# A decoder step on one Trainium2 core: the RWKV-7 chunk inverses' substitution on GpSimd, and projections in another order

## The chip, the core and the metric

The kernel runs on one core of a Trainium2 chip. The time is that of the whole kernel in device microseconds, from one launch. TensorE (PE) multiplies matrices, VectorE (DVE), ScalarE (ACT) and GpSimd (POOL) work element by element on 128 partitions, SyncE (SP) issues most DMAs. Each engine takes its own instructions strictly in order; between engines semaphores set what waits for what.

## What is computed

The reference is one inference step of a decoder of two layers (width 1024) on 512 prompt tokens and 8 x 4 sample tokens, 544 columns in all. Each layer has a SwiGLU block, a mixer and a second SwiGLU block. The mixer of the second (odd) layer is the one that the change touches: one input projection feeds a dilated window attention (8 heads: q, k, v) and an RWKV-7 time mixer (8 heads of 64). Cut to what matters:

```python
p = h @ odd_w_in[o]                       # q, k, v of the attention, then r, k, v, w, a, g of RWKV-7
def step(s, inp):                         # one token of RWKV-7, per head, s is 64 x 64
    r_t, w_t, k_t, v_t, kk_t, a_t = inp
    sk = jnp.einsum('bhvk,bhk->bhv', s, kk_t)
    s = (s * w_t[:, :, None, :] - sk[..., None] * (kk_t * a_t)[:, :, None, :]
         + v_t[..., None] * k_t[:, :, None, :])
    return s, jnp.einsum('bhvk,bhk->bhv', s, r_t)
s_final, ys = lax.scan(step, s0, seq)
...
mix = jnp.concatenate([att, yd], -1) @ odd_w_out[o]
```

All values are float32. A float32 matmul is made from three matmuls of split operands (high x high, high x low, low x high).

## The kernel before

**Projections.** A strip is 128 output columns; its weight of 1024 x 128 comes by DMA as `raw` (L446), ScalarE rounds it to `wh` (L448), VectorE takes the rest `wl` (L449), and TensorE runs three matmuls for each of 8 slices of the inner dimension, once for each half of the 544 columns (L460 to L462). So a half strip is 24 matmuls of 128 x 272. In the odd mixer there are 14 strips of RWKV-7 (x0 to x3 is r of the four head pairs, x4 to x7 is k, x8 to x11 is v, x12 and x13 the low-rank inputs; functions `xmixes`, `xmix`), 4 slices of v of the attention (`vproj`, two half strips each, turned by L575 and L578 afterwards), and 4 groups hp of q and k (`odd_qk`, four half strips each).

**RWKV-7 in chunks.** The 512 prompt tokens are taken as 16 chunks of 32. The heads go in four pairs p = 0 to 3. For each pair the generator `rw_first(p)` does three parts, split by `yield`: decays, k and its norm; then the scaled vectors Q (from kk), R (from r) and KBf, and the chunk matrices MQ and GP (matmuls L1422, masks L1425), of which the part to be inverted goes through DRAM (`rab`) into `EA`, so that each of the 128 partitions holds one chunk of 32 x 32 in an order that suits; then the **substitution**: 31 steps of a multiply (L1440, into `rtm`) and a subtract (L1441) on `U`, each step on the result of the one before. U goes back through DRAM (`rtb`) into `TT`. Between the two, the third part also turns Q and KBf and projects v of the pair (x8+p), whose chunk form `rv` has one buffer, as `EA`, `U`, `MQ` and `KBf` have; `rtm` and the strips' border tile `pdb` have two.

`rw_inverse(p)` then multiplies with the inverse (first matmul L1498, which needs TT, QB, VU), and builds per chunk the transition `MT` (L1517, into a diagonal that GpSimd has written, L1449), the input `W`, the readout `RR` (L1526, onto a copy of R that GpSimd has made, L1448) and Y. After two pairs `rw_rec(g)` runs through the 16 chunks (L1544), and `rw_sample(p)` does the sample tokens.

**The order.** The body of `odd_mix` names the order p by p: the first parts of pair p+1, the third part of pair p, the second part of pair p+1, some groups of `odd_qk`, the inverse of pair p. A scheduler orders each engine's instructions by the order in which they are written (an earlier one has priority) and by when their operands and buffers come free, so instructions of several pairs stand interleaved on an engine. v of the attention is projected ahead of all pairs, its first slice within the low-rank part.

Of the kernel before, what the change touches and what calls it, by code (L numbers as in the profile page):

```python
# [26 lines left out]
class Kern:  # L27
# [1224 lines left out]
    def rw_setup(self, pL, pA, pE, p2, pJ):  # L1252
# [83 lines left out]
    def rw_first(self, p):  # L1336
# [49 lines left out]
        t = E()  # L1386
# [23 lines left out]
        V.tensor_tensor(chunks(QR[:, 1]), chunks(r), dv[:, :, 1:33], op=M)  # L1410
# [5 lines left out]
        for h2 in range(2):  # L1416
# [19 lines left out]
        for i in range(31):  # L1436
# [3 lines left out]
            V.tensor_tensor(tv, U[:, 0:nj, i:i + 1].to_broadcast([128, nj, 31 - i]), EA[:, i:i + 1, i + 1:32].to_broadcast([128, nj, 31 - i]), op=M)  # L1440
            V.tensor_tensor(U[:, 0:nj, i + 1:32], U[:, 0:nj, i + 1:32], tv, op=S)  # L1441
# [9 lines left out]
        self.turn(QB[:, 0], [QR[:, 0, 128 * i:128 * i + 128] for i in range(4)])  # L1451
# [20 lines left out]
        self.f[p] = QB, KB, VU, GP  # L1472
# [9 lines left out]
    def rw_inverse(self, p, QB, KB, VU, GP, kind="rs"):  # L1482
# [50 lines left out]
    def rw_rec(self, g, pool, pq):  # L1533
# [6 lines left out]
        for n in range(1, 16):  # L1540
# [479 lines left out]
```

## Time and profile before

| | us |
|---|---|
| three runs | 2569.62, 2573.84, 2588.95 |
| median | 2573.84 |
| profiled execution | 2567.64 |
| its span on the core | 2565.8 |
| TensorE busy | 2442.6 (95%) |
| VectorE busy | 1232.4 (48%) |
| ScalarE busy | 943.3 (37%) |
| GpSimd busy | 409.0 (16%) |

The span is that of the trace, from the first instruction to the last; the profiled execution is one run and has its own time. Busy times of TensorE are modelled ends of pipelined matmuls. "PEclk" is the clock that TensorE was granted, as a share of the full one. The odd mixer's part with the four pairs lies between about 1643 and 1957 us. A row of the timeline gives the start in the span, the duration, the engine, the line, what it writes and reads, and in brackets how long the engine was idle before and what ended it.

### The profile page before, as it was taken

To read this page: it belongs to the slowest core of one execution; us is meant where nothing else is said; L and a number is where in the kernel's file an instruction comes from. 1 tells how busy PE (TensorE), PEld (TensorE's weight loads), DVE (VectorE), ACT (ScalarE), POOL (GpSimd) and SP (SyncE) were. 2 spreads that over 40 slices of the span, in tenths; PEclk is the share of its full clock that TensorE was granted. 3 is DMA by queue.
4 is the path that set the end of the run, shared out by engine and by line. 5 is a ranking of instruction groups with operands and counts; after the bars stand their busy time and mean duration, and the time that the engine had idled before them with its cause. 6 is when DMAs were issued, how large, how long until landed. Compare 5 with 4: busy or idle time off the path is not lost.

```text
span 2565.8 us, 50682 instructions
## 1 busy us (share of the span) xinstructions
PE 2442.6 (95%) x20338; PEld 2253.4 (88%) x20338; DVE 1232.4 (48%) x2999; ACT 943.3 (37%) x2051; POOL 409.0 (16%) x616
## 2 busy tenths in 40 slices
PE   6999999899899999999999999889999999999996
PEld 4988999897588999999989999878877578999996
DVE  6532356544577333345423334558664567333343
ACT  4322323435555333224323322545422545333222
POOL 1000016411432000031000003312111122000032
PEclk8999999999999999999999999889988999999998
DMA  7666335567632222223562232322322632222221
GB/s 237 203 217 216 113 118 112 188 216 252 222 122 75 87 88 94 80 80 105 173 222 83 85 91 81 103 77 78 92 75 92 211 113 74 87 89 94 80 80 58
DMA packets 184027, 318.27 MB, mean 124 GB/s; under 512 B 38416, under 2 KB 47040, under 8 KB 183664
## 3 DMA queue, kind: packets, MB, share of 16 engines
q1 hardware_dynamic: 172096, 282.52, 34.6%
q0 software_dynamic: 10400, 31.06, 4.1%
q8 instruction: 159, 2.61, 0.4%
q10 hardware_dynamic: 1296, 1.46, 0.2%
q14 instruction: 76, 0.62, 0.1%
HBM read 288.68 MB, written 26.28 MB: 123 GB/s over the span
## 4 chain that ended last, share of the span: by engine, by line
PE 82%; DVE 7%; DMA 4%; ACT 4%; issue 1%; POOL 1%; SPq 1%; ACTq 0%; POOLq 0%; DVEq 0%
PE mm L460 23%; PE mm L462 23%; PE mm L461 22%; PE ps L185 2%; DVE x L347 1%; DMA ar<-in_ada_w 1%; DMA raw<-in_ada_w 1%; ACT t L249 1%; DVE wl L449 1%; PE sc L1178 1%; PE sc L1156 1%; PE ad L185 1%; PE ps L460 1%; PE ps L462 1%; PE ps L461 1%
## 5 line engine op out<-in xcount | busy, mean ns | idle before, releaser
L460 PE MATMUL mm<-xh,wh 128*128 128x272 f32 x3720 | 1089.4, 295 | 35.5 <-ACT xh L250 10.1
L461 PE MATMUL mm<-xl,wh 128*128 128x272 f32 x3720 | 1082.7, 291 | 2.0 <-DVE xl L251 2.0
L462 PE MATMUL mm<-xh,wl 128*128 128x272 f32 x3720 | 1083.0, 292 | 0.8 <-DVE wl L449 0.8
L460 PEld LDWEIGHTS mm<-xh,wh 128*128 128x128 f32 x3720 | 706.0, 190 | 85.2 <-ACT t L401 31.2
L449 DVE TENSOR_TENSOR wl<-raw,wh 128x512 fp32r<-128x512 f32 (+1 forms) x664 | 458.8, 703 | 537.0 <-ACT wh L448 505.0
L461 PEld LDWEIGHTS mm<-xl,wh 128*128 128x128 f32 x3720 | 710.5, 191 | 7.0 <-DVE xl L251 2.5
L462 PEld LDWEIGHTS mm<-xh,wl 128*128 128x128 f32 x3720 | 706.6, 190 | 7.8 <-issue 4.2
L448 ACT ACTIVATE wh<-raw 128x512 fp32r<-128x512 f32 (+1 forms) x664 | 401.5, 618 | 727.6 <-PE mm L461 565.9
L460 PE MATMUL mm<-hh,wh 128*128 128x272 f32 x1280 | 370.4, 289 | 0.0
L462 PE MATMUL mm<-hh,wl 128*128 128x272 f32 x1280 | 370.4, 289 | 0.0
L461 PE MATMUL mm<-hl,wh 128*128 128x272 f32 x1280 | 369.5, 289 | 0.0
L460 PEld LDWEIGHTS mm<-hh,wh 128*128 128x128 f32 x1280 | 241.4, 189 | 0.8 <-issue 0.4
L461 PEld LDWEIGHTS mm<-hl,wh 128*128 128x128 f32 x1280 | 241.2, 188 | 0.4
L462 PEld LDWEIGHTS mm<-hh,wl 128*128 128x128 f32 x1280 | 241.1, 188 | 0.4
L402 DVE TENSOR_TENSOR t<-t,mm 128x272 f32<-128x272 f32 x169 | 73.4, 434 | 279.6 <-ACT t L401 279.4
L401 ACT ACTIVATE t<-mm 128x272 f32<-128x272 f32 x169 | 65.6, 388 | 318.6 <-PE mm L462 318.6
L297 POOL TENSOR_TENSOR sa<-x 128x272 f32<-128x272 f32 x24 | 26.1, 1087 | 907.4 <-DVE x L291 852.0
L291 DVE SCALAR_TENSOR_TENSOR x<-mm,rg,x 128x272 f32<-128x272 f32 (+1 forms) x96 | 45.9, 479 | 171.4 <-PE mm L462 170.7
L466 DVE TENSOR_TENSOR hl<-t,hh 128x272 fp32r<-128x272 f32 x160 | 69.6, 439 | 35.8 <-ACT hh L465 35.3
L465 ACT ACTIVATE hh<-t 128x272 fp32r<-128x272 f32 x160 | 67.5, 426 | 38.5 <-DVE t L402 38.5
L277 POOL TENSOR_TENSOR sq<-sq,t 128x272 f32<-128x272 f32 x60 | 54.7, 926 | 18.1 <-ACT t L276 17.3
L249 ACT ACTIVATE t<-x,S,G 128x272 f32<-128x272 f32 (+1 forms) x80 | 44.5, 589 | 24.1 <-DVE x L348 23.5
(643 smaller groups left out, 2536.6 us busy)
## 6 DMA issues: line engine op xcount, KB each, us to landing
raw<-in_ada_w SPq DMA_DIRECT2D x192, 256.0 KB
raw<-in_wg SPq DMA_DIRECT2D x176, 256.0 KB
raw<-in_wu SPq DMA_DIRECT2D x176, 256.0 KB
raw<-in_wd SPq DMA_DIRECT2D x160, 256.0 KB
ar<-in_ada_w SPq DMA_DIRECT2D x96, 256.0 KB
raw<-in_odd_rw SPq DMA_DIRECT2D x28, 256.0 KB
xs<-x POOLq DMA_DIRECT2D x16, 272.0 KB, 4.0
x<-xs POOLq DMA_DIRECT2D x8, 544.0 KB, 7.8
```

The source lines that it names most:

```text
L185: return nc.tensor.matmul(ps[32 * j:32 * j + 32], self.c32[:, 9 * k:9 * k + 32], r, start=(k == 0), stop=(k == 7))
L249: nc.scalar.activation(t[:, 0:n], x[:, d, c0:pe], AF.Identity, scale=G[:, d, 0:1], bias=S[:, d, 0:1])
L277: G.tensor_tensor(s["q"], s["q"], t, op=A)
L401: self.act = nc.scalar.activation(s, pss[2 * i], AF.Silu)
L402: mul = nc.vector.tensor_tensor(s, s, pss[2 * i + 1], op=ALU.mult)
L448: nc.scalar.activation(wh[:, 0:w], r[:, 0:w], AF.Copy)
L449: (lo or nc.vector).tensor_tensor(wl[:, 0:w], r[:, 0:w], wh[:, 0:w].bitcast(F32), op=ALU.subtract)
L460: nc.tensor.matmul(ps, wh[:, s], mh, start=first, stop=False)
L461: nc.tensor.matmul(ps, wh[:, s], ml, start=False, stop=False)
L462: self.last = nc.tensor.matmul(ps, wl[:, s], mh, start=False, stop=last)
L465: self.nc.scalar.activation(hi, src, AF.Copy)
L466: return (lo_eng or self.nc.vector).tensor_tensor(lo, src, hi.bitcast(F32), op=ALU.subtract)
```

## The change

1. The 62 instructions of the substitution of each pair are issued to GpSimd (G) instead of VectorE (V).
2. The copy of R into RR is gone. Q and R stand in a ring of three slots, R in slot 0 or 2, and the addition L1526 reads R from there. 
3. GpSimd's product that writes the diagonal MT moves from the third part of `rw_first` to the head of `rw_inverse`, and the buffers of a group of two pairs are taken there.
4. v of the attention is no longer projected ahead of the pairs: 0, 1, 1 and 2 of its four slices are drawn in pairs 0 to 3, and its output DMAs go behind. The groups of q and k move by one pair: none, 0, 1, 2 instead of 0, 1, none, 2.
5. The chunk loop of `rw_rec` is written under a higher priority.
6. The pool of scratch tiles has 8 buffers instead of 9, and one scratch tile (t) takes the place of `cum`, which is dead by then.

Other lines move by one: L1441 and L1442 are the substitution of the changed kernel, L1499 the first matmul of the inverse.

```diff
-        t = E()
+        t = cum
...
-        QR = pJ.tile([128, 2, SP], F32, name="rQR")
+        Q, R, QR = self.RQR[:, 1], self.RQR[:, 2 * (p % 2)], self.RQR[:, p % 2:p % 2 + 2]
...
-            V.tensor_tensor(tv, U[:, 0:nj, i:i + 1].to_broadcast([128, nj, 31 - i]), EA[:, i:i + 1, i + 1:32].to_broadcast([128, nj, 31 - i]), op=M)
-            V.tensor_tensor(U[:, 0:nj, i + 1:32], U[:, 0:nj, i + 1:32], tv, op=S)
+            G.tensor_tensor(tv, U[:, 0:nj, i:i + 1].to_broadcast([128, nj, 31 - i]), EA[:, i:i + 1, i + 1:32].to_broadcast([128, nj, 31 - i]), op=M)
+            G.tensor_tensor(U[:, 0:nj, i + 1:32], U[:, 0:nj, i + 1:32], tv, op=S)
...
-        if p % 2 == 0:
-            self.rw_group()
-        G.tensor_copy(self.RR[:, p % 2].rearrange("p n t -> p (n t)"), QR[:, 1])
-        G.tensor_tensor(self.MT[:, p % 2], self.id2.unsqueeze(1).to_broadcast([128, 16, 64]), DC[:, p, 0:16].unsqueeze(2).to_broadcast([128, 16, 64]), op=M)
...
+        if pg == 0:
+            self.rw_group()
+        full = [128, 16, 64]
+        nc.gpsimd.tensor_tensor(self.MT[:, pg], self.id2.unsqueeze(1).to_broadcast(full), self.DC[:, p, 0:16].unsqueeze(2).to_broadcast(full), op=M)
...
-            V.tensor_tensor(rr, rr, pr[par][:, 0:256].rearrange("p (n t) -> p n t", n=8), op=A)
+            V.tensor_tensor(self.RR[:, pg, par::2], R.rearrange("p (n t) -> p n t", n=16)[:, par::2], pr[par][:, 0:256].rearrange("p (n t) -> p n t", n=8), op=A)
...
-        for n in range(1, 16):
+        with self.tc.high_priority(offset=3000):
+          for n in range(1, 16):
...
-            self.rw_setup(pL, pA, pool("rke", 9, ea), p2, pJ)
+            self.rw_setup(pL, pA, pool("rke", 8, ea), p2, pJ)
...
-            for _ in self.vproj(self.vt, D["odd_v"], self.E, lambda: self.bank["ro"].tile([128, 512], F32, name="ro"), early):
-                pass
+            v = self.vproj(self.vt, D["odd_v"], self.E, lambda: self.bank["ro"].tile([128, 512], F32, name="ro"))
...
-                for h in ((0,), (1,), (), (2,))[p]:
+                for _ in range((0, 1, 1, 2)[p]):
+                    next(v)
+                for h in ((), (0,), (1,), (2,))[p]:
                     self.odd_qk(h, pQ)
```

On TensorE, six half strips (x8, x1, x6) stand between the chunk matrices of pair 0 and its first matmul on the inverse, where nine stood (x8, x1, four of q and k, one of x6). Ahead of pair 0's chunk matrices the eight of v are gone.

GpSimd, in the middle of pair 0's substitution (`rtm`, `rU`), in the changed kernel: L1397 is a product of pair 1's sample columns that reads kk (`e`), L1455 the copy of pair 0's v into its chunk form.

```order
L1442 TENSOR_TENSOR rU<-rU,rtm 128x5x15
L1397 TENSOR_TENSOR rSM<-e 128x32
L1441 TENSOR_TENSOR rtm<-rU,rEA 128x70
L1318 COPY dsh<-pdb 128x1
L1319 COPY dsh<-pdb 128x8
L1442 TENSOR_TENSOR rU<-rU,rtm 128x5x14
L1441 TENSOR_TENSOR rtm<-rU,rEA 128x65
L1455 COPY rv<-e 128x16x32
L1454 COPY rSM<-e 128x32
L1301 MEMSET pdb 128x1
L1302 COPY pdb<-c_rw_sh 128x8
L1442 TENSOR_TENSOR rU<-rU,rtm 128x5x13
```

Ahead of the first row stand 33 instructions of the substitution (the first row is the 34th), and the copy `rv` comes after the 37th; in the kernel before, none of these rows of `rtm` and `rU` is on GpSimd.

VectorE, pair 1's first half beside pair 0's substitution, in the kernel before (`e` are scratch tiles, `wl` the low part of a weight):

```order
L1320 SCALAR_TENSOR_TENSOR e<-pdb,c_rw_mu,e 128x32
L1401 SCALAR_TENSOR_TENSOR e<-e 128x544
L1441 TENSOR_TENSOR rU<-rU,rtm 128x5x12
L1410 TENSOR_TENSOR rQR<-e 128x512
L1402 TENSOR_TENSOR rKBf<-e 128x16x32
L1409 SCALAR_TENSOR_TENSOR e<-e,c_rw_par 128x544
L1440 TENSOR_TENSOR rtm<-rU,rEA 128x66
L1462 TENSOR_TENSOR e<-e,ps 128x272 x2
L1441 TENSOR_TENSOR rU<-rU,rtm 128x6x11
L449 TENSOR_TENSOR wl<-raw,wh 128x512
```

And in the changed kernel, the same part of pair 1: L1396 writes Q, L1398 is kk*=a in place, L1320 and L1321 mix the next strip, L1407 works on the sample columns.

```order
L1396 TENSOR_TENSOR rRQR<-e 128x512
L1320 SCALAR_TENSOR_TENSOR e<-pdb,c_rw_mu,e 128x512
L1321 SCALAR_TENSOR_TENSOR e<-pdb,c_rw_mu,e 128x32
L1398 TENSOR_TENSOR e<-e 128x544
L1399 TENSOR_TENSOR rKBf<-e 128x16x32
L1401 TENSOR_SCALAR e<-e,c_rw_par 128x544
L1402 SCALAR_TENSOR_TENSOR e<-e 128x544
L1403 TENSOR_TENSOR rKBf<-e 128x16x32
L1407 SCALAR_TENSOR_TENSOR rSM<-rSM,rDC 128x32
L449 TENSOR_TENSOR wl<-raw,wh 128x512 x2
L1320 SCALAR_TENSOR_TENSOR e<-pdb,c_rw_mu,e 128x512
L1321 SCALAR_TENSOR_TENSOR e<-pdb,c_rw_mu,e 128x32
```

The substitution's rows are gone between them; L1398 overwrites what GpSimd's L1397 reads, and L1407 reads what its L1400 leaves.

SyncE, behind pair 0's substitution (`rtb` carries U out, `rTT` brings the inverse in, `rab` and `rEA` are the way of pair 1's chunk matrices), in the kernel before:

```order
L1463 DMA vbd<-e 128x512
L446 DMA raw<-in_odd_rw 128x512 x2
L1444 DMA rtb_19782<-rU 256x1x32 x4
L1428 DMA rab_20079<-rMQ 32x16x32 x2
L1445 DMA rTT<-rtb_19782 128x8x32
L1434 DMA rU<-in_rU 128x256
L446 DMA raw<-in_odd_rw 128x512
```

And in the changed kernel:

```order
L1460 DMA vbd<-e 128x512
L1445 DMA rtb_19482<-rU 256x1x32 x4
L446 DMA raw<-in_odd_qk 128x512 x2
L1446 DMA rTT<-rtb_19482 128x8x32
L1435 DMA rU<-in_rU 128x256
L1429 DMA rab_19772<-rMQ 32x16x32 x2
L1433 DMA rEA<-rab_19772 32x1024 x4
L446 DMA raw<-in_odd_qk 128x512
```

The four writes of `rtb` still stand ahead of `rab` and `rEA` of the next pair; weights of q and k stand among them now.

## Rows read from the trace of the kernel before

**Rows 1.** Page: busy time of each engine; shares of the chain

```profile
PE 2442.6 (95%) x20338; PEld 2253.4 (88%) x20338; DVE 1232.4 (48%) x2999; ACT 943.3 (37%) x2051; POOL 409.0 (16%) x616
PE 82%; DVE 7%; DMA 4%; ACT 4%; issue 1%; POOL 1%; SPq 1%; ACTq 0%; POOLq 0%; DVEq 0%
```

**Rows 2.** Windows: five stretches of the mixer, columns as named

```profile
core 0: us, PE busy (x) PEld busy (x) DVE busy (x) ACT busy (x) POOL busy (x), PEclk, DMA share, GB/s
1643.00:1711.00 68.00, 61.89 (x480) 59.48 (x480) 33.77 (x64) 34.47 (x71) 15.26 (x39) 0.90 0.35 117
1711.00:1761.00 50.00, 44.42 (x401) 39.87 (x401) 37.68 (x104) 24.43 (x49) 12.94 (x28) 0.86 0.28 74
1761.00:1815.00 54.00, 51.57 (x744) 45.76 (x742) 41.94 (x133) 24.26 (x53) 10.60 (x25) 1.00 0.30 86
1815.00:1871.00 56.00, 53.94 (x780) 46.15 (x777) 33.83 (x104) 24.79 (x53) 7.18 (x22) 0.97 0.23 67
1871.00:1957.00 86.00, 77.13 (x1154) 67.54 (x1150) 50.42 (x154) 20.40 (x48) 16.51 (x26) 0.76 0.29 87
```

**Rows 3.** Timeline, TensorE: start, duration, work [idle before, releaser]

```profile
1760.51 1.26 PE L1498 MATMUL rs<-rQB,rTT 32*64 32x128 f32 x25
1814.67 0.55 PE L1498 MATMUL rs<-rQB,rTT 32*64 32x128 f32 x6
1882.81 0.48 PE L1519 MATMUL rs<-rVU,rKB 64*64 64x64 f32 x4 [1.28 <-DVE rMT L1517]
1887.81 0.43 PE L1523 MATMUL rs<-rGP,rTQ 64*64 64x32 f32 x4 [2.11 <-ACT rW L1521]
1934.89 0.48 PE L1498 MATMUL rs<-rQB,rTT 32*64 32x128 f32 x2 [3.07 <-DMA rTT<-rtb]
```

**Rows 4.** Timeline, TensorE, projection matmuls in a row in two stretches

```profile
1648.81 0.43 PE L462 MATMUL mm<-xh,wl 128*128 128x272 f32 x1
1649.04 0.43 PE L460 MATMUL mm<-xh,wh 128*128 128x272 f32 x1
...
1652.61 0.29 PE L460 MATMUL rx<-xh,wh 128*128 128x272 f32 x1
1652.73 0.29 PE L461 MATMUL rx<-xl,wh 128*128 128x272 f32 x1
```

**Rows 5.** Timeline, VectorE and GpSimd around pair 0's substitution

```profile
1711.36 0.42 DVE L1425 TENSOR_TENSOR rMQ<-ps,c_rmask 128x256 f32<-128x256 f32 x1 [0.60 <-PE ps L1422]
1718.48 1.18 DVE L1440 TENSOR_TENSOR rtm<-rU,rEA 128x31 f32<-128x31 f32 x1 [3.13 <-DMA rEA<-rab]
1717.71 1.90 POOL L1449 TENSOR_TENSOR rMT<-rid,rDC 128x1024 f32<-128x1024 f32 x1
```

**Rows 6.** Timeline, SyncE's queue behind pair 0's substitution

```profile
1751.97 2.60 SPq L1444 DMA_DIRECT2D rtb<-rU  x4
1754.67 1.07 SPq L1428 DMA_DIRECT2D rab<-rMQ  x2
1755.99 0.38 SPq L1445 DMA_DIRECT2D rTT<-rtb  x1
1757.58 0.84 SPq L1432 DMA_DIRECT2D rEA<-rab  x2
```

**Rows 7.** The two lines of the substitution on VectorE, minimum/median/maximum in ns

```profile
L1440 DVE TENSOR_TENSOR rtm<-rU,rEA x124: 163/214/1178, 1718.5 to 1926.0; 128x60 f32<-128x60 f32 x12, 128x28 f32<-128x28 f32 x8, 128x54 f32<-128x54 f32 x8, 128x48 f32<-128x48 f32 x8
L1441 DVE TENSOR_TENSOR rU<-rU,rtm x124: 171/214/612, 1719.7 to 1927.1; 128x60 f32<-128x60 f32 x12, 128x28 f32<-128x28 f32 x8, 128x54 f32<-128x54 f32 x8, 128x48 f32<-128x48 f32 x8
```

**Rows 8.** Groups by line, TensorE, 1643 to 1711: v's transposes

```profile
L575 PE MATMUL ro<-c_cst,e 128*128 128x128 f32 x16 | 2.7, 272 | 0.0
L578 PE MATMUL ro<-c_cst,e 128*32 128x128 f32 x4 | 1.1, 275 | 0.0
```

**Rows 9.** Timeline, GpSimd, two dependent products of 128x32 at two places

```profile
1786.99 0.26 POOL L1403 TENSOR_TENSOR rSM<-e 128x32 f32<-128x32 f32 x1
1787.32 0.24 POOL L1405 TENSOR_TENSOR rSM<-rSM,rDC 128x32 f32<-128x32 f32 x1
...
1890.99 0.76 POOL L1403 TENSOR_TENSOR rSM<-e 128x32 f32<-128x32 f32 x1 [1.85 <-DVE gnq L1247]
1891.82 0.61 POOL L1405 TENSOR_TENSOR rSM<-rSM,rDC 128x32 f32<-128x32 f32 x1
```

More of the change, by code (lines that the diff above doesn't have):

```diff
@@ L1271, in rw_setup @@
             nc.gpsimd.tensor_copy(self.id2[o:o + 64], self.ident[o:o + 64, o:o + 64])
+        self.RQR = t("rRQR", [128, 3, SP], pJ)
         self.TT = t("rTT", [128, 2, 4, 64], pJ)
@@ L1409, in rw_first @@
         V.scalar_tensor_tensor(bo, r, col("rk"), k, op0=M, op1=M)
-        V.tensor_tensor(chunks(QR[:, 1]), chunks(r), dv[:, :, 1:33], op=M)
+        V.tensor_tensor(chunks(R), chunks(r), dv[:, :, 1:33], op=M)
         G.tensor_tensor(smv(3), smp(r), ds[:, :, 1:5], op=M)
@@ L1424, in rw_first @@
                 mk = self.rc["rmask"][:, i].unsqueeze(1).unsqueeze(1).to_broadcast([128, 4, 2, 32])
-                V.tensor_tensor(dst[:, h2], pv[:, :, i].rearrange("p (q k) t -> p q k t", k=2), mk, op=M)
+                V.tensor_tensor(dst[:, h2], pv[:, :, i ^ 1 - p % 2].rearrange("p (q k) t -> p q k t", k=2), mk, op=M)
         ab = self.dr.tile([2, 8, 2, 32, 32], F32, name=f"rab{p}")
@@ L1445, in rw_first @@
         nc.sync.dma_start(self.TT.rearrange("p h k t -> p (h k) t")[:, :, 32:64], tb.rearrange("(n c) j t -> (c j) n t", c=4))
-        if p % 2 == 0:
-            self.rw_group()
-        G.tensor_copy(self.RR[:, p % 2].rearrange("p n t -> p (n t)"), QR[:, 1])
-        G.tensor_tensor(self.MT[:, p % 2], self.id2.unsqueeze(1).to_broadcast([128, 16, 64]), DC[:, p, 0:16].unsqueeze(2).to_broadcast([128, 16, 64]), op=M)
         QB = pJ.tile([128, 2, 4, 128], F32, name="rQB")
-        self.turn(QB[:, 0], [QR[:, 0, 128 * i:128 * i + 128] for i in range(4)])
+        self.turn(QB[:, 0], [Q[:, 128 * i:128 * i + 128] for i in range(4)])
         Kf = KBf.rearrange("p c a t -> p c (a t)")
@@ L1471, in rw_first @@
         V.tensor_copy(QB[:, 1].rearrange("p k (h v) -> p k h v", h=2), pv)
-        self.f[p] = QB, KB, VU, GP
+        self.f[p] = QB, KB, VU, GP, R
     def rw_group(self):
@@ L1480, in rw_group, with rw_inverse @@
         self.Y = t("rY", [128, 8, 2, 64])
-    def rw_inverse(self, p, QB, KB, VU, GP, kind="rs"):
+    def rw_inverse(self, p, QB, KB, VU, GP, R, kind="rs"):
         nc = self.nc
@@ L1686, in odd_mix @@
             nc.vector.tensor_scalar(self.omu, self.mu, -1.0, 1.0, op0=ALU.mult, op1=ALU.add)
-            self.rw_setup(pL, pA, pool("rke", 9, ea), p2, pJ)
+            self.rw_setup(pL, pA, pool("rke", 8, ea), p2, pJ)
             pQ = pool("oqk", 1, side="right")
             self.rw_lora()
-            early = {}
-            for s, k in zip(range(1), ('rx',)):
-                src = D["odd_v"][s].rearrange("p k n -> p (k n)")
-                w = [self.tile512(src[:, o:o + 512], lambda n: self.rp[0].tile([128, 512], F32R, name=n, tag="e"), None) for o in (0, 512)]
-                early[s] = self.proj(None, 0, w, bank=lambda: self.bank[k].tile([128, 512], F32, name=k))
             self.f = {}
@@ L1712, in odd_mix @@
                     next(f[p + 1])
-                for h in ((0,), (1,), (), (2,))[p]:
+                for _ in range((0, 1, 1, 2)[p]):
+                    next(v)
+                for h in ((), (0,), (1,), (2,))[p]:
                     self.odd_qk(h, pQ)
+                if p == 3:
+                    for _ in v:
+                        pass
+                    nc.sync.dma_start(D["c_v"][0:512].rearrange("(t p) n -> p t n", p=128), self.vt[:, 0:4])
+                    nc.sync.dma_start(D["c_v"][512:544], self.vt[0:32, 4])
                 self.rw_inverse(p, *self.f[p])
```

5 lines of the change are left out of this document (1 added, 4 removed).

## The prediction

> **What bounds the kernel now.** I read the page's busy shares first: TensorE works 95% of the span and 82% of the chain that ended last is its own [rows 1]. So time is gained only where TensorE stops or runs at its lower clock. All that the change touches lies in the odd layer's mixer, so I read the windows from 1643 to 1957 us next [rows 2]. The reader sees there that VectorE is busy 37.68 of 50 us while pair 0's substitution runs (1711 to 1761), and that the clock is at its two worst values there (0.86) and in the last stretch (0.76); the middle stretches run at 1.00 and 0.97 with 2.4 and 2.1 us idle. A clock of 0.76 over 86 us costs about 0.24 x 86 = 21 us, its idle time 8.9 us more. What lowers the clock is seen at the inverse of the last pair: TensorE waits 3.07 us for the inverse's way through DRAM (rTT<-rtb) [rows 3], and behind that it runs small matmuls only. The price of the clock: two projection matmuls in a row start 0.23 us apart at the lower level (1.2 GHz) and 0.12 to 0.13 us at the full one (2.4 GHz) [rows 4], so a half strip (24 of them) is 3.0 us at full clock.
>
> Then I read the steps of one inverse. The masks of pair 0's chunk matrices start at 1711.36, the first substitution op at 1718.48 (7.1 us for two trips through DRAM) [rows 5, 9]; the four writes of the result leave at 1751.97 [rows 6], so the substitution took 33.5 us, and the first matmul on the inverse starts at 1760.51 [rows 3], 8.6 us behind. Its 62 ops cost VectorE 163 to 214 ns each [rows 7]; by the medians that is 13 us a pair, so 20 us of the 33.5 are other VectorE work in between.
>
> **The change part by part.**
>
> *v leaves the front.* Eight half strips, 192 matmuls, 8 x 3.0 = 24 us, and their transposes (2.7 us and one us for the sample rows, 4 in all [rows 8]) no longer stand ahead of pair 0's masks. TensorE was busy 61.89 of 68 us there [rows 2], so I count all 28: the masks come at 1711.4 - 28 = 1683.4. This is no gain: the 28 us are owed, they now follow in pairs 2 and 3. Nor are qk's strips gone: the half strips (12 us) that stood in pair 0 stand in pair 1, and so on; by the inverse of pair 1 the new program owes 24 + 4 + 12 = 40 us of TensorE work against the old.
>
> *Pair 0's substitution on GpSimd.* No substitution op on GpSimd is in the trace. The nearest rows are its two dependent products of 128x32: alone they take 0.26 and 0.24 us and start 0.33 us apart; beside VectorE's long ops they take 0.76 and 0.61 and start 0.83 apart [rows 9]. Against its product of 128x1024 in 1.90 us [rows 5] that is about 0.18 us plus 1.68 ns an element. The 31 steps have 1560 elements on one partition, 50 a step, so 0.267 us, and 0.08 of gap (0.07 in the free pair, taken a little higher): 0.347 x 62 = 21.5 us. That is the lower bound. The upper: every op at the disturbed spacing, less the same allowance, 0.75 x 62 = 46.5 us. Between them I count VectorE's time in ops with two operands from SBUF while pair 0 runs: of the 20 us of other VectorE work above I take two thirds, 13 us, because casts, scans and reads of PSUM are among it. Then 21.5 + 13 = 34.5, and 20 other GpSimd instructions stand among the 62 (order) at about 0.26 us: 5 us. In all 39.5 us where VectorE took 33.5. I take that and not a bound, because VectorE is about 60% busy in this stretch less the substitution.
>
> The trace shows the exclusion from the other side too: VectorE's first substitution op took 1.18 us, where the median is 0.214, while GpSimd's 1.90 us product ran [rows 5, 7]. The Trainium skill, SBUF — State Buffer, section Who interferes with whom, says that a VectorE instruction with two SBUF inputs contends with a GpSimd instruction that reads SBUF, and that whoever issues first holds the shared ports for the whole instruction. The rows agree. By that rule the extra lies between nothing and VectorE's two-input time, which is how it is counted above.
>
> So the substitution starts at 1683.4 + 7.1 = 1690.5 and ends at 1730.0; with the same 8.6 us behind it the first matmul on the inverse is at 1738.6, 22 us earlier than before. But what covers it is less: six half strips (x8, x1, x6: 18 us) and small matmuls stand between the masks and that matmul, where nine stood. TensorE will be idle for 20 us or so there, and pay with its clock.
>
> *The trips of pair 1, and what is queued behind GpSimd.* SyncE's queue has rtb of pair 0 ahead of rab and rEA of pair 1, as before, so pair 1's substitution still starts some 11 us behind the end of pair 0's (before: 2.7 us for four writes, then rab at 1754.67 and rEA at 1757.58 [rows 6]). It starts at 1738.6 + 2.5 and takes 30 us (21.5, 5 of other instructions and less contention, since VectorE waits more). Two waits are new (line numbers of the changed kernel, as in the order). VectorE's kk*=a of the next pair overwrites what GpSimd's L1397 reads, and L1397 stands behind 34 substitution ops of pair 0 and 51 of pair 1; behind it on VectorE stand the mix of the next strip (L1320) and the sum RR (L1526), for whose bank TensorE's next group waits. And GpSimd's copy rv of pair 1 stands behind pair 1's whole substitution, at about 1738.6 + 37; the turns of VU wait for it, and behind them TensorE still has the half of x2, four half strips of qk0 and the small work of the sample, about 29 to 32 us. So the inverse of pair 1 is not 54 us behind that of pair 0, as in [rows 2, 3], nor 51 (one half strip less), but 69: 1807.6, against 1814.67 before.
>
> *RR copy, diagonals, ring, pool of 8.* The removed copy and the moved product are GpSimd's (1.90 us for the latter [rows 5]), and GpSimd had time: 7 to 17 us a stretch [rows 2]. In the new program MT stands ahead of the first substitution and costs nothing, since the trips hide it. For pairs 2 and 3 it waits for rec(0) to free the buffer and 45 substitution ops of pair 3 stand behind it; pair 3 is covered by six half strips of v and four of qk. Without that cover it would cost the wait of TensorE there, up to 6 us. The scratch pool of 8 instead of 9 I count at nothing (its tile t reuses one that is dead); if a strip waited for it, it would cost one such step, about 1 us a pair.
>
> *The rest.* Before, from 1814.67 to 1957 it was 142.3 us: 11.0 idle and about 22 for the clock (0.24 x 86 and 0.03 x 56) [rows 2], so 109 of work. After: 109 + 40 - 2 = 147, and what a covered stretch loses, 3 of 55 us, so 8; the waits for MT and W (1.28 and 2.11 us [rows 3]) stay, with some lower clock: 0 to 6. So 155 to 161, and it ends at 1962.6 to 1968.6, 6 to 12 us later than before; I take 8. The gain at pair 3 (some 25 us) and the loss at pairs 0 and 1 (idle 20, then 15) nearly cancel.
>
> The profiled execution took 2567.64 us, 6.2 less than the median of the three runs. Its own sum is 2567.6 + 8 = 2575.6; at the median 2573.84 + 8 = 2582.
>
> **The rivals.**
> *A. GpSimd is hardly disturbed* (0.35 us an op): 13 us less for pair 0, and pair 1 is not held, 51 instead of 69 us. 2582 - 13 - 18 = 2551; with only one of the two about 2566. For it: the free pair [rows 9]. Against: L1397 and rv stand where they stand.
> *B. Each op waits for a VectorE instruction.* 46.5 + 5 = 51.5 us a pair: 12 later in pair 0, 21 in pair 1; 2582 + 33 = 2615. For it: all the disturbed rows, 0.61 to 0.76 us against 0.25 [rows 9]. Against: VectorE is idle 40% of the time. The point from which it is slower by over 1% is 18 us more than I count, 9 a pair: a mean spacing of 0.70 us an op.
> *C. GpSimd takes twice VectorE's time, no more:* 0.42 us an op, 26 + 5 us, 8 less in pair 0, about the same in pair 1: 2574, no change. The rows put the ratio for short ops between 0.25 / 0.21 and 0.76 / 0.21.
> The Trainium skill, GPSIMD Engine Reference, section 4.1 Engine selection, has VectorE for elementwise work and GpSimd about 2x slower with two inputs. No run here shows that for the substitution. It is C's case, and it speaks against the change where the substitution is not covered.
>
> **How the numbers follow.** Forecast 0.45 (its own range 2570 to 2595), C 0.15, A 0.17, B 0.23. 1% is 25.7 us, about what a measurement of this kernel can tell from no change. Faster by over 1% (under 2548) is only the far end of A: 0.07. Slower by over 1% (above 2599.6) is most of B: 0.18. Within 1%: 0.75. The range drops the ends of A and B: 2554 to 2611.
>
> **What would show it.** The masks of pair 0 near 1683; substitution ops on GpSimd 0.45 to 0.65 us apart in pair 0; TensorE idle some 20 us ahead of the first matmul on pair 0's inverse, near 1739; pair 1's near 1808; no wait for rTT at pair 3 and a clock above 0.9 in the last stretch. I am wrong if pair 0's substitution is under 30 us or over 48, if pair 1's inverse comes within 55 us of pair 0's, or if the clock stays down behind pair 0.

## The result, and the profile after

Over 17 runs of each kernel the median went from 2581.77 to 2597.29 us. The ratio is 1.0062, with an interval of 1.005 to 1.0075: 16 us slower, clear of noise, and less than 1%. The forecast of 8 us had the sign; it had half the size. One of the changed kernel's 17 runs took 4237.22 us at a mean clock of 0.75; it is left out of the ratio.

The page of the changed kernel, span and busy times:

```profile
span 2600.3 us, 50704 instructions
PE 2449.7 (94%) x20338; PEld 2247.9 (86%) x20338; DVE 1192.5 (46%) x2751; ACT 946.7 (36%) x2053; POOL 485.5 (19%) x860
```

GpSimd is busy 485.5 us instead of 409.0 and VectorE 1192.5 instead of 1232.4; TensorE runs the same 20338 matmuls as in [rows 1], in 7 us more of busy time.

The profiled execution took 2602.28 us, 34.6 more than the one of before, and half of that is not the change. The windows of both kernels from 640 to 730 us, in the even layer where the programs are alike (first the kernel before, then the changed one; the columns are as in [rows 2]):

```profile
640.00:730.00 90.00, 79.18 (x555) 52.13 (x555) 49.79 (x177) 58.21 (x145) 31.74 (x42) 0.96 0.54 174
```

```profile
640.00:730.00 90.00, 79.18 (x465) 47.93 (x462) 39.94 (x149) 46.91 (x118) 28.79 (x38) 0.79 0.55 177
```

The granted clock was 0.96 in the one and 0.79 in the other. Of the changed kernel's delay 3.4 us are there at 612 us, 7.6 at 667 and 18.2 at 722; shortly ahead of the mixer it is 18.4. All positions of changed kernels below are therefore counted from a ScalarE instruction shortly ahead of the mixer that all programs have; for the changed kernel that means 18.4 us less than its trace shows, for the experiments 2.9 to 19.4 us less. What is then left at the end, 16.0 us, agrees with the ratio. Rows of timelines are shown with the times of their own trace.

The windows of the changed kernel that answer to [rows 2], shifted by 18.4, and a sixth one of 121 us behind them:

```profile
1661.40:1729.40 68.00, 50.13 (x340) 45.05 (x340) 31.55 (x60) 38.91 (x77) 27.95 (x77) 0.77 0.25 79
1729.40:1779.40 50.00, 38.24 (x497) 34.57 (x498) 26.66 (x46) 21.93 (x45) 33.03 (x92) 0.80 0.21 59
1779.40:1833.40 54.00, 45.05 (x584) 39.38 (x586) 23.85 (x47) 18.60 (x41) 27.72 (x79) 0.91 0.29 85
1833.40:1889.40 56.00, 55.74 (x853) 48.08 (x846) 32.36 (x70) 20.53 (x47) 22.45 (x65) 1.00 0.26 73
1889.40:1975.40 86.00, 84.86 (x1184) 75.94 (x1183) 40.29 (x79) 28.03 (x65) 32.12 (x77) 0.98 0.37 117
1975.40:2096.40 121.00, 107.91 (x899) 63.21 (x897) 64.07 (x222) 57.87 (x155) 12.80 (x36) 0.97 0.49 159
```

The sixth of the kernel before:

```profile
1957.00:2078.00 121.00, 114.52 (x877) 67.33 (x876) 64.29 (x222) 58.56 (x163) 13.99 (x36) 0.97 0.47 156
```

Two things are to be seen. In the front and at pairs 0 and 1, TensorE does less (50.13 of 68 us, 38.24 of 50, 45.05 of 54) at a lower clock (0.77, 0.80, 0.91). At pairs 2 and 3 it is busy throughout at 1.00 and 0.98, where the last stretch had 0.76. That is the exchange that was forecast. The last row was not: in the 121 us behind the inverses TensorE is busy 107.91 us instead of 114.52, at the same clock.

TensorE's larger waits in the timeline of the changed kernel, in the mixer and behind it, with the first matmul on pair 1's inverse (1823.89) among them:

```profile
1665.34 0.59 PE L460 MATMUL mm<-xh,wh 128*128 128x272 f32 x1 [8.01 <-ACT pdb L1311]
1705.37 3.32 PE L1423 MATMUL ps<-rRQR,rKBf 64*64 64x64 f32 x64 [5.37 <-DVE rKBf L1403]
1717.42 0.59 PE L460 MATMUL mm<-xh,wh 128*128 128x272 f32 x1 [4.70 <-ACT pdb L1311]
1731.75 0.39 PE L460 MATMUL mm<-xh,wh 128*128 128x272 f32 x1 [2.36 <-ACT pdb L1311]
1758.87 1.54 PE L1499 MATMUL rs<-rQB,rTT 32*64 32x128 f32 x13 [9.22 <-DMA rTT<-rtb]
1793.17 3.10 PE L1528 MATMUL rs<-rVU,rGP 64*32 64x64 f32 x54 [8.95 <-DVE rRR L1526]
1823.89 1.37 PE L1499 MATMUL rs<-rQB,rTT 32*64 32x128 f32 x28
1971.66 1.91 PE L1520 MATMUL rs<-rVU,rKB 64*64 64x64 f32 x64 [0.71 <-DVE rMT L1518]
2085.59 0.59 PE L549 MATMUL sm<-rKB,sPT 128*32 128x512 f32 x1 [1.75 <-issue]
2092.52 1.06 PE L549 MATMUL sm<-rKB,sPT 128*32 128x512 f32 x1 [3.45 <-DMA rKB<-in_ccv]
```

It waits 8.01 us at a projection, because the banks are emptied by ScalarE's copies into the border tiles; 5.37 for KBf ahead of pair 0's masks; 9.22 for pair 0's inverse; 8.95 for the sum RR. Pair 1's inverse begins without a wait, and no wait for rTT is left at pair 3. The last two rows lie in the attention of the sample tokens.

GpSimd and VectorE at the 8.95 us, one row each of their timelines:

```profile
1787.75 0.25 POOL L1397 TENSOR_TENSOR rSM<-e 128x32 f32<-128x32 f32 x1
1788.04 0.75 DVE L1398 TENSOR_TENSOR e<-e 128x544 f32<-128x544 f32 x1 [8.13 <-POOL rSM L1397]
```

VectorE was idle 8.13 us until GpSimd's L1397, which stood behind 55 substitution ops of pair 1 (the prediction counted 51); the sum RR came 4.7 us behind that, at 1792.71.

The two lines of the substitution on GpSimd, and five of its ops in a row in pair 0:

```profile
L1441 POOL TENSOR_TENSOR rtm<-rU,rEA x124: 199/294/1179, 1717.3 to 1916.4; 128x60 f32<-128x60 f32 x12, 128x28 f32<-128x28 f32 x8, 128x54 f32<-128x54 f32 x8, 128x48 f32<-128x48 f32 x8
L1442 POOL TENSOR_TENSOR rU<-rU,rtm x124: 211/297/844, 1718.8 to 1917.1; 128x60 f32<-128x60 f32 x12, 128x28 f32<-128x28 f32 x8, 128x54 f32<-128x54 f32 x8, 128x48 f32<-128x48 f32 x8
```

```profile
1726.62 0.32 POOL L1442 TENSOR_TENSOR rU<-rU,rtm 128x60 f32<-128x60 f32 x1
1727.02 0.32 POOL L1441 TENSOR_TENSOR rtm<-rU,rEA 128x76 f32<-128x76 f32 x1
1727.41 0.69 POOL L1442 TENSOR_TENSOR rU<-rU,rtm 128x76 f32<-128x76 f32 x1
1728.18 0.64 POOL L1441 TENSOR_TENSOR rtm<-rU,rEA 128x72 f32<-128x72 f32 x1
1728.90 0.68 POOL L1442 TENSOR_TENSOR rU<-rU,rtm 128x72 f32<-128x72 f32 x1
```

The median is 294 to 297 ns against 214 on VectorE [rows 7]. An op that is not disturbed takes 0.32 us for 60 to 76 elements, a disturbed one 0.64 to 0.69. From the start of the first op at 1717.27 to the end of the last at 1751.25, pair 0 took 34.0 us (VectorE: 33.5); the four pairs took 34.0, 26.8, 26.7 and 30.9 us, against 33.4, 28.5, 21.0 and 21.1 before.

### The profile page after: what moved, and what is told of

It is laid out like the page before. It is cut to its first block, busy times and chain, and to the rows that moved or that the text cites. A ratio compares the mean times of both kernels' runs of the same rounds, so it can differ in the third digit from the quotient of the medians.

```text
span 2600.3 us, 50704 instructions
## 1 busy us (share of the span) xinstructions
PE 2449.7 (94%) x20338; PEld 2247.9 (86%) x20338; DVE 1192.5 (46%) x2751; ACT 946.7 (36%) x2053; POOL 485.5 (19%) x860
## 4 chain that ended last, share of the span: by engine, by line
PE 82%; DVE 6%; DMA 4%; ACT 3%; POOL 3%; issue 1%; SPq 1%; another core or an unknown queue 0%; ACTq 0%; POOLq 0%; DVEq 0%
PE mm L460 23%; PE mm L462 22%; PE mm L461 22%; PE ps L185 2%; DVE x L347 1%; POOL rtm L1441 1%; POOL rU L1442 1%; DVE wl L449 1%; DMA raw<-in_ada_w 1%; ACT t L249 1%; PE sc L660 1%; PE sc L1156 1%; PE ad L185 1%; PE sc L1178 1%; DVE x L348 1%
## 5 line engine op out<-in xcount | busy, mean ns | idle before, releaser
L460 PE MATMUL mm<-xh,wh 128*128 128x272 f32 x3728 | 1093.1, 295 | 43.4 <-ACT pdb L1311 18.4
L299 POOL TENSOR_TENSOR sa<-sa,x 128x272 f32<-128x272 f32 x36 | 28.7, 800 | 146.1 <-DVE x L295 79.8
```

Of the source, the lines that this page charges most:

```text
L460: nc.tensor.matmul(ps, wh[:, s], mh, start=first, stop=False)
```

## The experiments

Each run is timed against the kernel before on the same chip. The table gives the ratio, the end of the last inverse (last matmul of L1528, aligned as above) against the kernel before, and the stretch from there to one and the same matmul of the next block. The kernel before has 208.3 us there. Both columns are worked out from the one profiled execution of each kernel. The ratios do not always give what these columns add up to: six of the kernels (e2, e4, e5, e7, e8, e9) lose 3 to 4 us more by the ratio, e11 and e15 about 7.5 us more, the others agree within 1.5 us. Why is open, so a difference of a few us in these columns alone proves nothing.

| kernel | ratio [interval] | end of last inverse | stretch behind it |
|---|---|---|---|
| changed | 1.0062 [1.005, 1.0075] | +4.1 | 220.2 |
| e1: substitution on VectorE again | 1.0073 [1.006, 1.0087] | +5.2 | 220.6 |
| e2: before, substitution on GpSimd | 1.0054 [1.004, 1.0068] | +10.9 | 207.9 |
| e4: projections in the old order | 1.0106 [1.0091, 1.0122] | +24.1 | 208.4 |
| e5: nothing waits behind GpSimd | 1.0037 [1.0023, 1.005] | -1.7 | 215.4 |
| e6: e5 without priority | 1.009 [1.0073, 1.0106] | +18.2 | 214.5 |
| e7: e5, v's stores later | 1.005 [1.0035, 1.0064] | -2.7 | 220.7 |
| e8: e5, v spread | 1.0006 [0.9997, 1.0015] | -0.4 | 206.6 |
| e9: before, projections moved | 1.0023 [1.0014, 1.0032] | +3.7 | 206.9 |
| e10: e8, q and k in old places | 1.0037 [1.0023, 1.0051] | +0.2 | 218.8 |
| e11: e8, early half strip of v | 1.002 [1.0009, 1.003] | -0.6 | 206.5 |
| e12: e2, nothing waits behind GpSimd | 1.0026 [1.0013, 1.0039] | +7.2 | 207.9 |
| e15: before, priority alone | 1.003 [1.0012, 1.0049] | -3.2 | 211.7 |

### e1, e2 and e4: one part undone, or one part alone

```diff
# e1, on the changed kernel
-            G.tensor_tensor(tv, U[...], EA[...], op=M)
-            G.tensor_tensor(U[:, 0:nj, i + 1:32], U[...], tv, op=S)
+            V.tensor_tensor(tv, U[...], EA[...], op=M)
+            V.tensor_tensor(U[:, 0:nj, i + 1:32], U[...], tv, op=S)
# e2, on the kernel before: the same two lines, V to G
# e4, on the changed kernel
-            v = self.vproj(...)
+            for _ in self.vproj(..., early): pass      # with early and the stores as before
-                for _ in range((0, 1, 1, 2)[p]):
-                    next(v)
-                for h in ((), (0,), (1,), (2,))[p]:
+                for h in ((0,), (1,), (), (2,))[p]:
```

> The changed kernel with the 62 substitution ops of each pair issued to VectorE again, all else as changed. Theory M (the substitution is as fast on GpSimd, 34.0 us against 33.5 in pair 0, and the loss is in what stands behind it on GpSimd and in the work that no longer covers pair 0): the 9 us that TensorE waits at pair 1 go, pair 0 stays uncovered, so 5 to 10 us less than the changed kernel, 6 to 11 us above the kernel before (ratio 1.002 to 1.004). Rival R1 (GpSimd is the whole loss): at or below the kernel before (ratio 1.000 or less). Rival R2 (the new order of the projections is the whole loss): it stays 16 us above (ratio 1.006).

> The kernel before with only the substitution issued to GpSimd; projections, diagonals and copies of R as before. Theory M: pair 0 is covered as before, the next pair's VectorE work waits behind GpSimd's queue in pairs 0 to 2 and the last pair stays uncovered: 5 to 10 us above the kernel before (ratio 1.002 to 1.004). R1: 16 us above (1.006). R2: no difference (1.000).

> The changed kernel with v of the attention projected ahead of the pairs again and the groups of q and k in their old places; substitution on GpSimd, diagonals late, R in the ring, priority for the chunk loop. Theory M: pair 0 is covered again (9 us of TensorE's wait go), the last pair is uncovered again (3 us of wait and some 20 us for the clock come back), pair 1 waits as in the changed kernel: 5 to 15 us above the kernel before. R2: at or below the kernel before. R1: 16 us above.

e1 gave 1.0073: with the substitution back on VectorE the rest of the change costs 19 us. So GpSimd is not the loss (R1 falls), but theory M's 5 to 10 us gain did not come either. The wait of 8.95 us is gone, as M said: the inverse of pair 1 came 19.6 us earlier than before instead of 9.2. Yet TensorE then reached the end of the last inverse 5.2 us late and the stretch behind stayed at 220.6. No run shows where the lead of pair 1 was lost. The interval of e1 overlaps that of the changed kernel: with all else as changed, the two engines cannot be told apart.

e2 gave 1.0054, 14 us, more than M said and near R1's 1.006, which only e1 rules out. TensorE's larger waits in it, timeline:

```profile
1765.03 2.89 PE L1498 MATMUL rs<-rQB,rTT 32*64 32x128 f32 x32 [5.23 <-DMA rTT<-rtb]
1802.09 0.66 PE L1333 MATMUL ps<-c_cst,rv 128*128 128x128 f32 x3 [3.19 <-POOL rv L1458]
1950.88 1.51 PE L1498 MATMUL rs<-rQB,rTT 32*64 32x128 f32 x13 [5.10 <-DMA rTT<-rtb]
```

It waits 5.23 us for pair 0's inverse, 3.19 for rv behind GpSimd's substitution, 5.10 at the last pair, which has no cover here and whose substitution takes 24.8 us instead of 21.1.

e4 gave 1.0106, the slowest of all, so R2 falls with it. These 27 us are also more than M (5 to 15) and R1 (16) said. On top of the rest of the change the new order is worth 11 us (1.0106 to 1.0062), though alone it costs 6 (e9, below). TensorE's wait in it, and VectorE and GpSimd at the same place:

```profile
1909.35 2.57 PE L1520 MATMUL rs<-rVU,rKB 64*64 64x64 f32 x64 [12.42 <-DVE rMT L1518]
1908.61 1.28 DVE L1518 TENSOR_TENSOR rMT<-rMT,rs 128x512 f32<-128x512 f32 x2 [13.14 <-POOL rMT L1489]
1906.67 3.76 POOL L1489 TENSOR_TENSOR rMT<-rid,rDC 128x1024 f32<-128x1024 f32 x2
```

With the old order, pair 2's transition waits 12.42 us for the diagonal MT. The first chunk loop, which frees its buffer, has ended at 1894.5, but on GpSimd the diagonal stands behind 37 substitution ops of pair 3, from 1893.24 on. So this, too, is a wait for what is queued behind the substitution. In the changed kernel 17 ops stand ahead of the diagonal, and no such wait of pair 2 is left.

### e5 and e12: nothing behind the substitution on GpSimd

```diff
-        G.tensor_tensor(smv(0), smp(kk), ds[:, :, 0:4], op=M)
+        V.tensor_tensor(smv(0), smp(kk), ds[:, :, 0:4], op=M)
-        G.tensor_tensor(smv(6), smp(kk), smp(Dk), op=M)
+        V.tensor_tensor(smv(6), smp(kk), smp(Dk), op=M)
-        G.tensor_copy(self.rv[:, :, 0], chunks(v_))
+        V.tensor_copy(self.rv[:, :, 0], chunks(v_))
```

> The changed kernel with three of GpSimd's small instructions on VectorE: the two sample products that read and follow kk (L1397, L1400) and the copy of v into its chunk form (L1455), so that VectorE and TensorE wait for nothing that stands behind the substitution on GpSimd. Theory M: TensorE's 8.95 us wait at pair 1 goes, 7 to 9 us less than the changed kernel, 7 to 9 us above the kernel before (ratio 1.003). Rival: the wait only moves to the inverse of pair 1, since that waits for the same substitution: 16 us above (1.006).

> The kernel before with the substitution on GpSimd (as e2) and the three small instructions on VectorE that e5 moved, so that nothing waits behind the substitution on GpSimd. Theory M (the move costs by what stands behind it, 3.2 us at rv and 5 to 8 us at the next pair, and is neutral by itself): 7 to 10 us less than e2, ratio 1.001 to 1.003. Rival: the move by itself lengthens the last, uncovered pair, so e2's loss stays: ratio 1.005.

e5 gave 1.0037, 6 us less than the changed kernel, and e12 1.0026, 7 us less than e2; by the intervals each of these differences is uncertain by some 5 us. The timelines of e5 at the same places:

```profile
1775.43 2.00 PE L1528 MATMUL rs<-rVU,rGP 64*32 64x64 f32 x64 [1.87 <-DVE rRR L1526]
1771.80 0.29 DVE L1397 TENSOR_TENSOR rSM<-e 128x32 f32<-128x32 f32 x1
1772.13 0.73 DVE L1398 TENSOR_TENSOR e<-e 128x544 f32<-128x544 f32 x1
```

The wait for RR is 1.87 us instead of 8.95, since L1397 now runs on VectorE itself, 0.29 us ahead of L1398. Three instructions a pair, of 0.24 to 1.12 us each on GpSimd, were worth 6 to 7 us, in both orders of projections.

The move itself depends on the order. On the kernel before, e12 has nothing left behind the substitution and still costs 7 us, clear of noise, so M's "neutral by itself" falls there. TensorE waits in it for the inverses of pair 0 and of the last pair, where the kernel before has no wait and 3.07 us [rows 3]:

```profile
1776.97 2.25 PE L1498 MATMUL rs<-rQB,rTT 32*64 32x128 f32 x26 [5.54 <-DMA rTT<-rtb]
1961.51 2.89 PE L1498 MATMUL rs<-rQB,rTT 32*64 32x128 f32 x32 [4.93 <-DMA rTT<-rtb]
```

In the new order it is the other way: e5 against e1, the same order with the substitution on VectorE, is 9 us less.

### e6 and e15: the priority of the chunk loop

```diff
# e6, on e5
-        with self.tc.high_priority(offset=3000):
+        if True:
# e15, on the kernel before
-        for n in range(1, 16):
+        with self.tc.high_priority(offset=3000):
+          for n in range(1, 16):
```

> e5 without the higher priority of the chunk loop. In e5 the inverses end 2 us earlier than in the kernel before, and yet the attention behind them ends 5 us later: the stretch from the last inverse to a fixed matmul of the next block is 215 us against 208. Theory P (the priority puts the second chunk loop ahead of the attention's first matmuls, which then lag): the stretch goes back to about 208, 5 to 8 us less than e5, ratio about 1.001. Rival V (the late v does it): the stretch stays at 213 to 217 and the ratio at 1.003 to 1.005.

> The kernel before with the higher priority of the chunk loop and nothing else. Without it e5 lost 14 us (e6), most of it at pair 2, which waits for the first chunk loop. In the kernel before pair 2 waits 1.28 and 2.11 us there (rMT, rW) and runs at a low clock behind that. Theory P (the chunk loop's place is worth time in any of these programs): 3 to 8 us below the kernel before, ratio 0.997 to 0.999. Rival W (it is worth something only where the diagonals are written behind the chunk loop, as in the changed kernel): no difference, ratio 0.999 to 1.001.

e6 gave 1.009, so theory P falls: the stretch stayed at 214.5 us, as rival V said, but the kernel lost 14 us, which V did not say. Two rows of its timeline:

```profile
1913.70 0.42 PE L1524 MATMUL rs<-rGP,rTQ 64*64 64x32 f32 x2 [8.17 <-ACT rW L1522]
1911.16 0.63 ACT L1243 ACTIVATE ro<-rY 128x512 f32<-128x512 f32 x1 [10.31 <-DMA rob<-ro]
```

Pair 2 waits 8.17 us for W. ScalarE's copy into W (L1522) stands there behind L1243, an instruction of the readout that follows the first chunk loop, and that one waits 10.31 us for a DMA. The chunk loop itself ends 11 us later than in e5, and this L1243 comes 20 us later (aligned); in e5 it is done ahead of W. So without the priority the readout's trip falls into pair 2's inverse; the moved diagonals are not what is waited for here. e15 gave 1.003, slower than both theories said. Its inverses end 3.2 us early and the stretch behind them is 211.7 us, which about cancel in its profile; the ratio's lower end is 1.0012, and where the rest of it lies is not settled.

### e7 to e11: where the projections stand

```diff
# e7, on e5: the two stores of c_v behind the attention (self.ahead(units())) instead of at p == 3
# e8, on e5
+            next(v)
+            next(v)                                  # the first slice ahead of pair 0
-                for _ in range((0, 1, 1, 2)[p]):
-                    next(v)
+                for _ in range((1, 1, 1, 0)[p]):
+                    next(v, None)                    # stores at p == 2
# e9, on the kernel before: v, q and k and the stores as in the changed kernel, nothing else
# e10, on e8
-                for h in ((), (0,), (1,), (2,))[p]:
+                for h in ((0,), (1,), (), (2,))[p]:
# e11, on e8: early half strip of v through the bank rx, as in the kernel before
```

> e5 with the two output DMAs of v issued behind the attention instead of in pair 3. In e5 they stand on SyncE's queue at 1940 and 1943, right ahead of the first weights of the next modulation (1941 to 1944, against 1920 to 1923 in the kernel before), and TensorE waits 0.8 and 2.8 us for such weights later. Theory D (the stores push the weights): the two waits go, 3 to 5 us less than e5, ratio about 1.002. Rival: the place of these weights follows the matmuls ahead, so nothing moves: ratio 1.003 to 1.005.

> e5 with v's four slices spread over the front and pairs 0 to 2 instead of one in pair 2 and three in pair 3; stores of v behind pair 2. Theory V (the late v both uncovers the front and pair 0, where TensorE waits 7.7 and 7.8 us, and crowds the last pair): some 8 to 12 us of these waits are filled, and the stretch behind the inverses is again about 208 us instead of 215; 8 to 15 us less than e5, ratio 0.998 to 1.000. Rival: each half strip moved ahead delays the chain through the inverses by its own 3.0 us, so that nothing is won: ratio 1.003 to 1.005.

> The kernel before with v, q and k projected later as in the changed kernel, and nothing else: substitution on VectorE, diagonals and copies of R as before. With this run and e1, e2 and e4 the parts can be added up. Theory M: the front is 20 us shorter, 24 us are owed, pair 0 is uncovered, the last pair covered, the stretch behind the inverses is 12 us longer: 8 to 18 us above the kernel before (ratio 1.003 to 1.007). Rival: the cover of the last pair (about 25 us of wait and low clock) outweighs this: at or below the kernel before.

> e8 with the groups of q and k in their old places (0, 1, none, 2). In e8 TensorE still waits 7.8 us for pair 0's inverse and has to work through 13 us more by the inverse of pair 2. Theory C (only cover counts: work is conserved, and four half strips in pair 0 fill the wait): 5 to 8 us less than e8, ratio 0.997 to 0.999, the first sign of a gain over the kernel before. Rival Q (each half strip put ahead of an inverse delays all later ones by its 3.0 us and opens a wait at the last pair): ratio 1.000 to 1.003, with a wait for rTT at pair 3.

> e8 with v's first half strip in the low-rank part again, through the bank rx, as in the kernel before. In e8 TensorE waits 8.0 us at 1650 because both banks of the projections are full; a half strip through another bank takes 3.0 us of that for nothing. Theory C: 2 to 4 us less than e8, ratio 0.9985 to 1.000. Rival: the wait is of the chain through ScalarE and the front stays as long: ratio 1.0006, no change.

e7: 1.005, no gain. But the edit moved only one of the two stores. SyncE's queue in it:

```profile
1944.73 0.40 SPq L1747 DMA_DIRECT2D out_c_v<-vt  x1
1945.18 3.95 SPq L202 DMA_DIRECT2D ar<-in_ada_w  x4
1949.23 0.37 SPq L1748 DMA_DIRECT2D out_c_v<-vt  x1
```

The first store still stands right ahead of the weights, which start 1 us earlier than in e5 (aligned), and TensorE still waits 1.97 and 1.11 us for them. Theory D is not borne out, and was half tested.

e8: 1.0006 with an interval that holds 1. It is the best of all these, the same as the kernel before, 8 us below e5. But the way was not as expected in one half: the wait for pair 0's inverse is still there, and so is the one in the front,

```profile
1650.31 0.59 PE L460 MATMUL mm<-xh,wh 128*128 128x272 f32 x1 [8.01 <-ACT pdb L1311]
1745.72 1.54 PE L1499 MATMUL rs<-rQB,rTT 32*64 32x128 f32 x12 [7.79 <-DMA rTT<-rtb]
```

8.01 and 7.79 us. The gain is the stretch behind the inverses: 206.6 us, 8.8 less than in e5.

e9: 1.0023, 6 us, so the rival (no loss) falls. Its own sum lay at 8 to 18, too high: it counted 12 us for the stretch behind the inverses, which is 206.9 us here.

e10: 1.0037. The wait for pair 0's inverse is gone from its timeline, as theory C said, and the inverses end 0.2 us behind the kernel before; the stretch behind is 218.8 us. So neither of its theories names what happened. e11: 1.002, no gain over e8 by its profile nor by the times; the wait in the front is still 8.00 us, as its rival said.

### What the stretch behind the inverses goes with

The fourth column has two levels, and they do not follow any part of the change: 206.5 to 208.4 (before, e2, e4, e8, e9, e11, e12) and 211.7 to 220.7 (changed, e1, e5, e6, e7, e10, e15). TensorE over the whole stretch, first in the kernel before, then in the changed one (columns as in [rows 2]):

```profile
1955.68:2163.99 208.31, 196.78 (x1489) 146.53 (x1490) 126.12 (x356) 101.44 (x264) 48.88 (x77) 0.97 0.38 126
```

```profile
1978.24:2198.43 220.19, 200.82 (x1483) 148.07 (x1477) 126.75 (x357) 104.12 (x266) 47.80 (x77) 0.95 0.36 119
```

Of the 12 us, 8 are idle time of TensorE (19.4 us instead of 11.5) and 4 are longer busy time at a clock of 0.95 instead of 0.97. All kernels of the first level are idle 10.7 to 11.9 us there, all of the second 15.0 to 20.0.

The levels go with the order of TensorE's instructions. The attention's scores (L1156, 64 matmuls in the trace) and the sample attention's four rounds over the cached values (L549, eight matmuls a round) stand interleaved, in five orders. Numbers of scores ahead of the first round, between the rounds and behind the last:

| kernels | scores ahead, between, behind | stretch |
|---|---|---|
| before, e2, e9, e12 | 36, 4, 24, 0, 0 | 206.9 to 208.3 |
| e4, e8, e11 | 28, 4, 20, 0, 12 | 206.5 to 208.4 |
| changed, e1, e5, e7, e10 | 32, 4, 24, 0, 4 | 215.4 to 220.7 |
| e15 | 32, 4, 24, 4, 0 | 211.7 |
| e6 | 36, 0, 24, 4, 0 | 214.5 |

One part of the difference can be followed. In the seven kernels of the first level TensorE waits for no round; in the others it waits 1.1 to 5.5 us, 5.2 of them in the changed kernel (1.75 and 3.45, the last two rows of its timeline in the section on the result; the profile names no cause of the first). The first load for the last round, in the changed kernel and then in the kernel before, and the start of that round in the kernel before:

```profile
2086.64 0.33 SPq L1204 DMA_DIRECT2D rKB<-in_ccv  x1
```

```profile
2065.87 0.33 SPq L1204 DMA_DIRECT2D rKB<-in_ccv  x1
2070.71 0.62 PE L549 MATMUL sm<-rKB,sPT 128*32 128x512 f32 x1
```

In both kernels this load is issued some 1.05 us behind the start of the third round (2085.59 and 2064.79). The kernel before has 23 small matmuls of the attention (L1169, L1178) between the third round and the last, about 3 us, and the last begins without a wait; the changed kernel has four.

It is likely, and not shown, that the scheduler arrives at another order because the changes upstream move by a few us what comes free when. The match holds for 14 programs, but one order alone spreads over 5 us, and no run changed the order alone (e15, with the priority only, comes nearest). So it is not shown that the order is the whole of the 3 to 12 us.

## Why the prediction was right, and where it was not

**Direction: right, in part by luck.** The exchange that the sum described took place: a loss at the front and pairs 0 and 1, a gain at pair 3 (no wait for rTT, clock 0.98 instead of 0.76). But up to the last inverse it makes only 4.1 of the 16 us. The rest arose behind, where the sum has no term, and the range of 57 us was wide enough to hold both.

**v leaves the front: mis-sized.** The step said 28 us; the masks of pair 0 ended 21.1 us earlier than before. (The row at 1711.36 [rows 5] is the second of them; the first starts at 1710.00, which changes nothing here.) The eight half strips had filled waits. Without them TensorE waits 8.01 us at 1665 and 5.37 for KBf, where the timeline of the kernel before has 4.92 and 1.98:

```profile
1643.90 0.59 PE L460 MATMUL mm<-xh,wh 128*128 128x272 f32 x1 [4.92 <-ACT xh L465]
1708.13 3.18 PE L1422 MATMUL ps<-rQR,rKBf 64*64 64x64 f32 x64 [1.98 <-DVE rKBf L1402]
1720.52 0.60 PE L460 MATMUL mm<-xh,wh 128*128 128x272 f32 x1 [5.17 <-ACT pdb L1310]
```

**The substitution of pair 0: mis-sized.** 39.5 us against 34.0. The op alone was right (0.267 us and 0.08 of gap; undisturbed ops have a mean of 0.275). The extra for VectorE was not: 16 of the 62 ops took over 0.45 us, 11.7 us together, which is 7 us more than they would have taken at 0.28 to 0.30; I had 13. The Trainium skill, SBUF — State Buffer, section Who interferes with whom, calls the port pair that VectorE and GpSimd share an exclusive lock. The rows fit: disturbed ops take 0.64 to 1.06 us, 13 of the 16 at most 0.77, about an undisturbed one and half a VectorE instruction of 0.7.

The Trainium skill, GPSIMD Engine Reference, section 4.1 Engine selection, has GpSimd about 2x slower with two inputs. These short ops do not show that: 294 ns against 214 by the medians, 1.4x. What the move itself costs, e1, e5 and e12 answer differently for the two orders of projections.

**Pair 0's inverse: right, by two errors that cancel.** Forecast 1738.6, measured 1740.4. TensorE's wait for it is 9.22 us, and 4.70 and 2.36 us at the banks on the way there: 16 where I said some 20. But 5.17 us of a bank wait stood there before as well (last row above), so the change added 11.

**What is queued behind GpSimd: right.** From pair 0's inverse to pair 1's I had 69 us instead of 51; it took 65.0 us. The mechanism is the one named, L1398 behind L1397 and RR behind that, and e5 and e12 show its price: 6 to 7 us. The other wait that I named, for rv of pair 1, is not seen in the changed kernel; e2 has it, with 3.19 us.

**The rest: right to the last inverse.** I had its end 6 to 12 us late; it came 4.1 us late. The remark that the late diagonals cost up to 6 us without cover was too small: 12.42 us in e4. The priority has no term in the sum; without it e5 loses 14 us. And I laid the low clock of the last stretch before to the wait for rTT alone. In the trace of the kernel before the clock is 0.50 from 1937 to 1949, behind that wait, but also from 1883 to 1901, from pair 2's waits for MT and W on.

**Behind the last inverse: the step that failed.** The sum ended at 1957 and took everything behind as unchanged. That stretch became 12 us longer, which is three quarters of the 16 us: 8 us of TensorE's idle time and 4 of longer busy time. The work in it is nearly the same (1489 and 1483 matmuls); their order is not, and it stood in the program ahead of the run. How much of the 12 us the order makes is open.

**The rivals.** A (GpSimd hardly disturbed, pair 1 not held) did not happen: 16 of pair 0's 62 ops were disturbed and pair 1 was held. The second half of it is what e5 makes, and even that is 1.0037. B needs a mean spacing of 0.70 us; pair 0 has 34.0 us less 6.7 of others over 62, 0.44. C, no change, is 16 us off.

**The parts do not add up.** The substitution alone costs 14 us (e2), the projections alone 6 (e9), the whole 16. The projections cost 6 on the kernel before and save 11 on the rest of the change (e4 against the changed kernel), where they cover a last pair and diagonals that the other parts have made late: the waits of 12.42 us (e4) and 3.07 us (before, pair 3) are gone in the changed kernel.

## What to carry to other kernels

When a chain of short instructions is moved to an idle engine, list first what else stands in that engine's queue and who waits for it: three small bystanders cost 6 to 7 us here, and were moved away in three lines. What the chain itself costs depends on what covers it: with the queue cleared the move lost 7 us in the old order of projections (e12) and gained 9 in the new one (e5 against e1). Work that seems to be in the way ahead of a chain may be filling its waits; take it away and only part of its time comes back. And where a scheduler sets the order, read the order far behind the change too: most of this loss lay there, though it is not shown that the order made all of it.

## What the runs showed of the hardware that was not expected

One and the same code, the even layer from 640 to 730 us, ran at a granted clock of 0.96 in one execution and 0.79 in another. With 4 us from ahead of it that moved all that follows by 18 us; on a comparison of two single traces it would have doubled the loss. The experiments ran on two chips, and the level goes with the chip: 0.92 to 0.94 in the eight executions on the one (e1 to e9), 0.79 to 0.91 in the four on the other (e10 to e15), where the kernel before, too, has a median of 2580 to 2582 us instead of 2570. Which chip the first two traces are from is not on record. GpSimd takes these two-input ops of 8 to 76 elements in 0.20 to 0.33 us when undisturbed, where VectorE's minimum is 163 ns and its median 214 [rows 7]; most of that time, some 0.2 us, is there at any of these sizes. In the changed kernel 16, 11, 9 and 12 of the 62 ops of pairs 0 to 3 were disturbed (over 0.45 us).
